# Two of a late turn's four sums and their low parts on GpSimd, and convolution operands in one run per partition

## The chip, the cores and the metric

The kernel runs on one core of a Trainium2 chip. The metric is device time in microseconds, the median of several runs. A core has five engines that work side by side, each in its own order: TensorE (PE; its weight loads are listed as PEld), VectorE (DVE), ScalarE (ACT), GpSimd (POOL) and SyncE (SP), which issues nearly all DMAs here.

## The reference

One layer of a hybrid backbone: an adaptive RMSNorm of x (2048 tokens of 1024) and of a context (256 tokens), one input projection, a bidirectional gated linear scan over eight heads and a gated short convolution beside each other, an output projection and a final norm. Cut to what matters:

```python
h = rmsnorm(x, norm_w) * (1 + scale) + shift
p = h @ w_in                      # 1024 x 9216: 5 parts for the scan, 4 for the convolution
q, v, kf, gf, kb, gb = hgrn_prep(p[..., :HG_COLS], lb_f, lb_b)
o, _, _ = bidir_scan(q, kf, kb, v, gf, gb, s_f, s_b)   # s_f, s_b from the context
y_hg = hgrn_out(o, gate, onorm_w)
h_, bg, cg, gate2 = the other four parts of p
y_cv = bg * conv3(cg * h_, w) * silu(gate2)
y = concat(y_hg, y_cv) @ w_out
out = rmsnorm(x + gate * y, final_norm_w)
```

## The kernel before

**Products.** A float32 product is made from fp16 operands, each split into a high part (the value cast to fp16) and a low part (the value less the high part). Per 128 rows of the contraction TensorE makes three matmuls: high by high, high by low, low by high (L930 to L932 in `seven`). A product of 2 x 2 blocks is made from seven products of blocks instead of eight. The moving operands of the seven are `OPS`: B11, T1, T2, B21, T3, B22, T4, where T1 = b12 - b11, T2 = b22 - T1, T3 = b22 - b12 and T4 = b21 - T2, and b11 to b22 are blocks of the normalised rows, 256 tokens wide. The results go to four banks (sa, sb and others) and are evacuated by ScalarE (`p` and `u`, L937) and VectorE (`f`, `b` and others, L941).

**Turns.** The tokens come in four groups of 512 (`GW`; `HW` is half of it). Of each group the rows are normalised, transposed by TensorE (L274) and scaled; then a *turn* makes operands of them, one step per k of 0 to 3, each with the 128 features k of the upper and of the lower half. Groups 2 and 3 get *whole* turns (`turn`, `combine` with `whole`), which make all seven operands. Groups 0 and 1 are first used plain, as undivided high and low parts, and their rows `h` are kept in DRAM (`Xd`); the T operands come later, in *late* turns (`late_turn`), which load the rows again as `ha` and `hb` and make T1 to T4. There are eight whole turns, between 88 and 196 us of the profiled execution, and eight late ones, between 196 and 336 us. `ht` holds T1 and T2 side by side; T3 is written over b12 in `ha`, T4 over b21 in `hb`.

`store2` splits one or two operands: a cast to the high part (`cast`, on ScalarE at L303 or on GpSimd at L301, as its caller says), a subtraction on VectorE for the low part (L321), and a DMA of the pair tile `hp...` to DRAM by SyncE (L324, L326). The list `low` collects these subtractions so that another group's normalisation can be ordered behind them (`follow`). `prefetch` loads operands of a group from DRAM into the tiles `hop...` (L1389), once all four late turns of that group have been recorded.

**What sets the order.** The program is recorded as a row of units of matmuls. Beside the units run steps (turns, levels of the scan, norms), which `run` and `tick` spread over the matmuls by weights in the table `PACE`. A scheduler then orders each engine's instructions, and tiles come free by their pools. The scan of one head goes through levels: per level ScalarE makes a rearranged copy `km` of K (L601) and GpSimd one of Q, `qm` (L608; one buffer); VectorE updates K and Q (L485, L492); TensorE multiplies them into A (L631, L650), which ScalarE and GpSimd copy on (L661, L665).

**Convolution units.** From about 1335 us on, 28 units of 84 matmuls (2352) each cover two token groups at once: 512 columns, 256 from either group. Their operands `C0...` and `C1...` are loaded from `Hd` in DRAM by `load_C` (L986 to L993) into tiles that hold, for each of four k, the high and the low part of 512 columns. Later the same tiles hold the operands of w_out (`wo_home`, `wo_at`, `load_wo`).

Of the kernel before, what the change touches and what calls it, by code (L numbers as in the profile page):

```python
# [10 lines left out]
F16 = mybir.dt.float16  # L11
# [4 lines left out]
ALU = mybir.AluOpType  # L16
# [3 lines left out]
P = 128  # L20
# [5 lines left out]
GW = 512  # L26
NG = SEQ // GW
NCH = GW // P
HK = KT // 2
HW = GW // 2  # L30
# [30 lines left out]
def hybrid_layer(ctx: ExitStack, tc, x, cx, w_ada, b_ada, w_in, w_out, fnorm_w, small_d, masks, ident_d, sel_d, out):  # L61
# [179 lines left out]
    def norm_group(ntile, src, row0, m, nm, first_ops=None, space=q_tile):  # L241
# [72 lines left out]
        def store2(ops, k, row, eng):  # L314

            n2 = len(ops)
            pair = hp.tile([P, n2, 2, HW], F16, tag="pair", name=f"hp{ops[0]}_{nm}{k}", bufs=4)
            hi, lo = pair[:, :, 0], pair[:, :, 1]
            row = row.rearrange("p (a b) -> p a b", a=n2)
            cast(eng, hi, row)  # L320
            low.append(V.tensor_tensor(lo, row, hi, ALU.subtract))  # L321
            g = row0 // GW
            if n2 == 2:
                SY.dma_start(Hr[g][ops][:, :, k], pair)  # L324
            else:
                SY.dma_start(Hd[g][ops[0]][:, k], pair[:, 0])  # L326
# [30 lines left out]
        def combine(k, a, b, whole):  # L357
            b11, b12, b21, b22 = a[:, :HW], a[:, HW:], b[:, :HW], b[:, HW:]
            t = ring(f"ht_{nm}{k}")
            t1, t2 = t[:, :HW], t[:, HW:]  # L360
            V.tensor_tensor(t1, b12, b11, ALU.subtract)
            V.tensor_tensor(t2, b22, t1, ALU.subtract)
            store2(("T1", "T2"), k, t, S)
            V.tensor_tensor(b12, b22, b12, ALU.subtract)
            if whole:
                store2(("B11", "T3"), k, a, S)
                store2(("B21", "B22"), k, b, G)
            else:
                store2(("T3",), k, b12, S)
            V.tensor_tensor(b21, b21, t2, ALU.subtract)  # L370
            store2(("T4",), k, b21, G)

        return ([paced("load", lambda i=i: load(i)) for i in range(ntile)],
                [paced("square", lambda i=i: square(i)) for i in range(ntile)] + [paced("norm", norm)],
# [611 lines left out]
    def load_C(names, pool=None, tp=0):  # L986

        def one(o, j):
            if j == 0:
                C[tp][o] = (pool or ext.cr).tile([P, HK, 2, GW], F16, name=f"C{tp}{o}")  # L990
            SY.dma_start(C[tp][o][:, :, :, j * HW:(j + 1) * HW], Hd[2 * tp + j][o])

        return [lambda o=o, j=j: one(o, j) for o in names for j in range(2)]  # L993

# [64 lines left out]

    def wo_home(name, hl):  # L1060
        i = 2 * OPS.index(name) + hl
        return C[i // 7][OPS[i % 7]]

    def wo_at(name, hl, k):
        return wo_home(name, hl)[:, k // 2, k % 2, :]

    def load_wo(lo_, hi_):

        for i in range(lo_, hi_):
            SY.dma_start(wo_home(OPS[i // 2], i % 2).rearrange("p a k n -> p (a k) n"), Wd[OPS[i // 2]][:, i % 2])  # L1070

    Gr = dp.tile([P, GW], F32, name="Gr", tag="Gr")

# [377 lines left out]
    ui = 0  # L1451

    def run(wi, units, steps):
# [20 lines left out]
        for un, (wk, kind, i, fn) in enumerate(units):  # L1474
# [36 lines left out]
            elif kind == "pair":  # L1511
                def pair_step(o, last_unit=ui == len(uses) - 1):
                    tick(2)
                    if o and last_unit and o != OPS[6]:
                        load_wo(7 + OPS.index(o), 8 + OPS.index(o))

                seven(w.ops.get, lambda o, hl, k, i=i: C[i][o][:, k, hl, :], HK, GW, f"{ui}", pair_step,
                      w.sx[:, 0:1], ring, retire, *fn(w))
            else:
                def step(o, final=final):  # L1520
                    tick(1)
                    if o and final:
                        freed[0] += 1
                        prefetch()

                seven(w.ops.get, lambda o, hl, k: hop[gw][o][:, k, hl, :], HK, HW, f"{ui}", step,
                      w.sx[:, 0:1], u_tile, retire, *fn(w))
# [157 lines left out]
```

## Time and profile before

| | us |
|---|---|
| median of 3 runs | 2150.0 (2148.01 to 2152.14) |
| profiled execution | 2151.83 |
| its span | 2150.1 |
| TensorE busy | 2073.2 (96% of the span) |
| TensorE's weight loads busy | 1466.0 (68%) |
| VectorE busy | 1645.8 (77%) |
| ScalarE busy | 1192.2 (55%) |
| GpSimd busy | 191.8 (9%) |

The profiled execution's time is the span and 1.7 us around it. The mean granted clock of TensorE is 0.994 of full speed. The shares are means over the whole program; what VectorE, ScalarE and GpSimd do in a stretch, and what TensorE waits for there, is read from that stretch (the rows further down). A wait is listed by the waiting instruction and the one that ended last before it could start.

### The profile page before, as it was taken

The page shows a single profiled execution, that of the slowest core. Times are in us where ns is not written, and L with a number is a line of the kernel's source. Part 1 is how long each engine was busy: PE and PEld are TensorE (multiplying, and loading weights), DVE is VectorE, ACT ScalarE, POOL GpSimd, SP SyncE. Part 2 cuts the span into 40 slices and gives each one's busy share as a digit, 9 for nine tenths or more (in the row PEclk, how much of TensorE's full clock was granted, in tenths as well). Part 3 has the DMA queues.
Part 4 walks back from the last instruction along what each step waited for, and adds up shares of the span by engine and source line. Part 5 has one row for each costly group of instructions (what it writes and reads, how often), then busy time and mean ns, then how long its engine had stood idle before and what let it go on. Part 6 is the DMA issues. An engine that isn't in the chain of part 4 may idle for free.

```text
span 2150.1 us, 53050 instructions
## 1 busy us (share of the span) xinstructions
PE 2073.2 (96%) x22111; PEld 1466.0 (68%) x22111; DVE 1645.8 (77%) x3413; ACT 1192.2 (55%) x2406; POOL 191.8 (9%) x272
## 2 busy tenths in 40 slices
PE   5988999999999999999999999999999999999998
PEld 2877878888888888888888887444444444444443
DVE  6787988878778787788687887678778656687775
ACT  7965666757567666576676654354445423333332
POOL 0121111111111110111110100000000000000000
PEclk9999999999999999999999999999999999999999
DMA  9567533442344233424543458933442105642421
GB/s 356 191 207 265 178 126 134 137 158 72 114 129 146 97 114 109 153 81 142 194 131 127 130 165 260 285 108 110 134 149 93 54 23 196 206 143 92 137 79 59
DMA packets 185798, 311.02 MB, mean 145 GB/s; under 512 B 13010, under 2 KB 114770, under 8 KB 183764
## 3 DMA queue, kind: packets, MB, share of 16 engines
q1 hardware_dynamic: 183396, 303.68, 42.9%
q8 instruction: 173, 2.83, 0.5%
q10 hardware_dynamic: 2160, 3.93, 0.5%
q14 instruction: 69, 0.57, 0.1%
HBM read 240.19 MB, written 67.37 MB: 143 GB/s over the span
## 4 chain that ended last, share of the span: by engine, by line
PE 65%; DVE 18%; ACT 7%; DMA 4%; issue 3%; POOL 1%; SPq 0%; POOLq 0%; ACTq 0%; DVEq 0%
PE sa L930 8%; PE sa L932 8%; PE sa L931 8%; PE sb L930 4%; PE sb L932 4%; PE sb L931 4%; PE sa_o L930 2%; PE sa_o L931 2%; PE sa_o L932 2%; DVE Q L492 2%; PE sc L930 2%; PE sc L931 2%; PE sc L932 2%; DVE K L485 2%; PE T L681 2%
## 5 line engine op out<-in xcount | busy, mean ns | idle before, releaser
L931 PEld LDWEIGHTS <-e_p 128*128 128x128 f16 x1332 | 130.4, 98 | 59.8 <-issue 10.3
L930 PEld LDWEIGHTS <-e_p 128*128 128x128 f16 x1332 | 130.4, 98 | 54.0 <-issue 1.1
L601 ACT ACTIVATE km<-K 128x512 f32<-128x512 f32 x192 | 129.6, 675 | 67.2 <-DVE K L485 61.1
L932 PEld LDWEIGHTS <-e_p 128*128 128x128 f16 x1332 | 130.3, 98 | 51.4
L485 DVE TENSOR_TENSOR K<-K,tot 128x512 f32<-128x512 f32 x192 | 132.2, 689 | 42.9 <-ACT km L601 25.3
L492 DVE TENSOR_TENSOR Q<-Q,tot 128x512 f32<-128x512 f32 x192 | 132.5, 690 | 34.9 <-POOL qm L608 19.5
L608 POOL COPY qm<-Q 128x512 f32<-128x512 f32 x96 | 80.8, 842 | 794.4 <-DVE Q L492 778.7
L931 PEld LDWEIGHTS <-whib_p 128*128 128x128 f16 x888 | 86.9, 98 | 42.1 <-issue 8.8
L930 PEld LDWEIGHTS <-whib_p 128*128 128x128 f16 x888 | 86.8, 98 | 36.7 <-issue 0.8
L930 PEld LDWEIGHTS <-whia_p 128*128 128x128 f16 x888 | 87.0, 98 | 35.7 <-DMA hop3B<-Hd3B 2.3
L932 PEld LDWEIGHTS <-wloa_p 128*128 128x128 f16 x888 | 87.0, 98 | 34.2
L931 PEld LDWEIGHTS <-whia_p 128*128 128x128 f16 x888 | 87.0, 98 | 33.9 <-issue 1.5
L932 PEld LDWEIGHTS <-wlob_p 128*128 128x128 f16 x888 | 86.8, 98 | 34.0
L157 ACT ACTIVATE e_p<-ws_p,sc_p 128x512 f16<-128x512 f32 x108 | 77.5, 718 | 54.9 <-DVE ws_p L444 42.0
L665 POOL COPY A<-Ac 32x128 f32<-32x128 f32 x128 | 77.2, 603 | 128.3 <-ACT A L661 110.6
L853 ACT ACTIVATE cv<-c,small 128x512 f32<-128x512 f32 (+1 forms) x36 | 24.2, 673 | 106.8 <-DVE c L871 61.1
L937 ACT ACTIVATE u<-sa,sx_w 128x256 f32<-128x256 f32 (+1 forms) x111 | 58.1, 524 | 43.5 <-PE sa L932 34.7
L937 ACT ACTIVATE p<-sa,sx_w 128x256 f32<-128x256 f32 (+1 forms) x111 | 57.4, 517 | 39.9 <-PE sa L932 39.8
L158 DVE SCALAR_TENSOR_TENSOR e_p<-ws_p,sc_p,e_p 128x512 f16<-128x512 f32 x108 | 79.4, 750 | 0.0
L409 ACT ACTIVATE junk<-ws_p 128x1024 f16<-128x1024 f32 x72 | 75.7, 1052 | 6.5 <-DMA ws_p<-in_w_in 6.3
L1596 POOL TENSOR_TENSOR x_o<-x_o,fw 128x512 f32<-128x512 f32 x1 | 1.3, 1262 | 868.0 <-ACT junk L1587 868.0
L937 ACT ACTIVATE p<-sb,sx_w 128x256 f32<-128x256 f32 (+1 forms) x111 | 57.8, 521 | 30.8 <-PE sb L932 28.0
(858 smaller groups left out, 7036.3 us busy)
## 6 DMA issues: line engine op xcount, KB each, us to landing
ws_p<-in_w_in SPq DMA_DIRECT2D x72, 512.0 KB, 4.3
y_o<-yT SPq DMA_DIRECT2D x32, 512.0 KB, 4.3
xt_x<-in_x SPq DMA_DIRECT2D x16, 512.0 KB, 6.2
wa<-in_w_ada SPq DMA_DIRECT2D x16, 512.0 KB, 10.2
Gd<-zs SPq DMA_DIRECT2D x32, 256.0 KB, 2.7
sg<-Gd SPq DMA_DIRECT2D x32, 256.0 KB, 4.4
wos<-in_w_out SPq DMA_DIRECT2D x32, 256.0 KB, 5.0
yT<-y SPq DMA_DIRECT2D x32, 256.0 KB, 2.9
```

The source lines that it names most:

```text
L157: S.activation(hi, src, AF.Copy, scale=st[:, 0:1])
L158: V.scalar_tensor_tensor(lo, src, st[:, 0:1], hi, ALU.mult, ALU.subtract)
L409: S.activation(junk.rearrange("p (k n) -> p k n", k=KT), stage[i], AF.Abs, accum_out=r)
L485: V.tensor_tensor(m, m, sub(cur, nb + 1, [[2, np_], [-(nb + 1), 2], [0, B]]), ALU.mult)
L492: V.tensor_tensor(m, m, sub(cur, 1, [[2, np_], [nb - 1, 2], [0, B]]), ALU.mult)
L601: S.activation(sub(s.km, 0, [[2 * B, n // (2 * B)], [B, 2], [1, B]]), mix(s.K, n, B, n // (2 * B)), AF.Copy)
L608: G.tensor_copy(sub(qm, 0, [[2 * B, n // (2 * B)], [B, 2], [1, B]]), mix(s.qf, n, B, n // (2 * B)))
L665: G.tensor_copy(A3[js, :, js], s.Ac[js])
L930: PE.matmul(ps, hi[:, k], rh, start=start and k == 0, stop=False, skip_group_check=not start)
L931: PE.matmul(ps, hi[:, k], right(name, 1, k), start=False, stop=False, skip_group_check=not start)
L932: PE.matmul(ps, lo[:, k], rh, start=False, stop=k == nk - 1, skip_group_check=not start)
L937: last_keep.append(S.activation(r, ps, AF.Copy, scale=sx))
```

## The change

In `combine`, a late turn makes T3 and T4 on GpSimd (`eng`); a whole turn makes them on VectorE as before. T4's high part is always cast by ScalarE. In `store2`, the low part of an operand that is stored alone (T3 and T4 of a late turn, T4 of a whole one) is subtracted on GpSimd, and it is no longer in the list `low`. The tiles `C` hold the two token groups behind each other ([P, 2, HK, 2, HW] in place of [P, HK, 2, GW]), so that one load is one run of 4 KB per partition in place of eight runs of 512 B; the matmuls' moving operand is then two stretches of 256 columns. The homes of w_out's operands are the same bytes under another view.

```diff
@@ -318,7 +318,10 @@
             hi, lo = pair[:, :, 0], pair[:, :, 1]
             row = row.rearrange("p (a b) -> p a b", a=n2)
             cast(eng, hi, row)
-            low.append(V.tensor_tensor(lo, row, hi, ALU.subtract))
+            if n2 == 2:
+                low.append(V.tensor_tensor(lo, row, hi, ALU.subtract))
+            else:
+                G.tensor_tensor(lo, row, hi, ALU.subtract)
             g = row0 // GW
             if n2 == 2:
                 SY.dma_start(Hr[g][ops][:, :, k], pair)
@@ -361,14 +364,15 @@
             V.tensor_tensor(t1, b12, b11, ALU.subtract)
             V.tensor_tensor(t2, b22, t1, ALU.subtract)
             store2(("T1", "T2"), k, t, S)
-            V.tensor_tensor(b12, b22, b12, ALU.subtract)
+            eng = V if whole else G
+            eng.tensor_tensor(b12, b22, b12, ALU.subtract)
             if whole:
                 store2(("B11", "T3"), k, a, S)
                 store2(("B21", "B22"), k, b, G)
             else:
                 store2(("T3",), k, b12, S)
-            V.tensor_tensor(b21, b21, t2, ALU.subtract)
-            store2(("T4",), k, b21, G)
+            eng.tensor_tensor(b21, b21, t2, ALU.subtract)
+            store2(("T4",), k, b21, S)
 
         return ([paced("load", lambda i=i: load(i)) for i in range(ntile)],
                 [paced("square", lambda i=i: square(i)) for i in range(ntile)] + [paced("norm", norm)],
@@ -987,8 +991,8 @@
 
         def one(o, j):
             if j == 0:
-                C[tp][o] = (pool or ext.cr).tile([P, HK, 2, GW], F16, name=f"C{tp}{o}")
-            SY.dma_start(C[tp][o][:, :, :, j * HW:(j + 1) * HW], Hd[2 * tp + j][o])
+                C[tp][o] = (pool or ext.cr).tile([P, 2, HK, 2, HW], F16, name=f"C{tp}{o}")
+            SY.dma_start(C[tp][o][:, j], Hd[2 * tp + j][o])
 
         return [lambda o=o, j=j: one(o, j) for o in names for j in range(2)]
 
@@ -1059,15 +1063,15 @@
 
     def wo_home(name, hl):
         i = 2 * OPS.index(name) + hl
-        return C[i // 7][OPS[i % 7]]
+        return C[i // 7][OPS[i % 7]].rearrange("p j k l n -> p (j k l n)").rearrange("p (k n) -> p k n", n=GW)
 
     def wo_at(name, hl, k):
-        return wo_home(name, hl)[:, k // 2, k % 2, :]
+        return wo_home(name, hl)[:, k, :]
 
     def load_wo(lo_, hi_):
 
         for i in range(lo_, hi_):
-            SY.dma_start(wo_home(OPS[i // 2], i % 2).rearrange("p a k n -> p (a k) n"), Wd[OPS[i // 2]][:, i % 2])
+            SY.dma_start(wo_home(OPS[i // 2], i % 2), Wd[OPS[i // 2]][:, i % 2])
 
     Gr = dp.tile([P, GW], F32, name="Gr", tag="Gr")
 
@@ -1514,7 +1518,7 @@
                     if o and last_unit and o != OPS[6]:
                         load_wo(7 + OPS.index(o), 8 + OPS.index(o))
 
-                seven(w.ops.get, lambda o, hl, k, i=i: C[i][o][:, k, hl, :], HK, GW, f"{ui}", pair_step,
+                seven(w.ops.get, lambda o, hl, k, i=i: C[i][o][:, :, k, hl, :], HK, GW, f"{ui}", pair_step,
                       w.sx[:, 0:1], ring, retire, *fn(w))
             else:
                 def step(o, final=final):
```

In the fences below, the number behind a name is the tile's; line numbers of the changed kernel are three higher from L325 and four higher from L364 on. First GpSimd's queue at the first two late turns (k = 0 and 1 of the group `x1`), before:

```order
L608 COPY qm1_0_2_2732<-Q_0_2_2411 128x512
L608 COPY qm3_0_2_2847<-Q_0_2_2411 128x512
L301 TENSOR_SCALAR hpT4_x10_2635<-hb_x10_2619 128x256
L301 TENSOR_SCALAR hpT4_x11_2840<-hb_x11_2824 128x256
L608 COPY qm5_0_2_2970<-Q_0_2_2411 128x512
L665 COPY A_0_2_3029<-Ac_0_2_2695 32x4x32 x4
```

and of the change:

```order
L612 COPY qm1_0_2_2732<-Q_0_2_2411 128x512
L368 TENSOR_TENSOR ha_x10_2618<-hb_x10_2619,ha_x10_2618 128x256
L612 COPY qm3_0_2_2847<-Q_0_2_2411 128x512
L374 TENSOR_TENSOR hb_x10_2619<-hb_x10_2619,ht_x10_2622 128x256
L324 TENSOR_TENSOR hpT3_x10_2630<-ha_x10_2618,hpT3_x10_2630 128x256
L324 TENSOR_TENSOR hpT4_x10_2635<-hb_x10_2619,hpT4_x10_2635 128x256
L368 TENSOR_TENSOR ha_x11_2823<-hb_x11_2824,ha_x11_2823 128x256
L374 TENSOR_TENSOR hb_x11_2824<-hb_x11_2824,ht_x11_2827 128x256
L324 TENSOR_TENSOR hpT3_x11_2835<-ha_x11_2823,hpT3_x11_2835 128x256
L612 COPY qm5_0_2_2970<-Q_0_2_2411 128x512
L324 TENSOR_TENSOR hpT4_x11_2840<-hb_x11_2824,hpT4_x11_2840 128x256
L669 COPY A_0_2_3029<-Ac_0_2_2695 32x4x32 x4
```

The two casts of T4 are gone; two sums (L368, L374) and two low parts (L324) per turn have come between the copies `qm1`, `qm3` and `qm5`.

ScalarE at the first late turn, before:

```order
L601 ACTIVATE km4_0_2_2850<-K_0_2_1859 128x512
L303 ACTIVATE hpT1_x10_2625<-ht_x10_2622 128x2x256
L303 ACTIVATE hpT3_x10_2630<-ha_x10_2618 128x256
L937 ACTIVATE p1_17_2864<-sa_17_2807,sx_w2_690 128x256
L542 ACTIVATE f_0_3_2573<-sa_16_2575,sx_w0_482 128x256
L523 ACTIVATE f_0_3_2573<-f_0_3_2573,lb_125,lb1_126 128x512
L538 ACTIVATE f_0_3_2573<-f_0_3_2573 128x512
L524 ACTIVATE K_0_3_2574<-f_0_3_2573 128x512
L523 ACTIVATE f_0_3_2573<-f_0_3_2573,lb_125,lb1_126 128x512
```

and of the change (`f_0_3` are evacuations and updates of the scan's gates, `p1_17` an evacuation of bank sa):

```order
L605 ACTIVATE km4_0_2_2850<-K_0_2_1859 128x512
L303 ACTIVATE hpT1_x10_2625<-ht_x10_2622 128x2x256
L303 ACTIVATE hpT3_x10_2630<-ha_x10_2618 128x256
L303 ACTIVATE hpT4_x10_2635<-hb_x10_2619 128x256
L542 ACTIVATE f_0_3_2573<-f_0_3_2573 128x512
L941 ACTIVATE p1_17_2864<-sa_17_2807,sx_w2_690 128x256
L527 ACTIVATE f_0_3_2573<-f_0_3_2573,lb_125,lb1_126 128x512
L546 ACTIVATE f_0_3_2573<-sa_16_2575,sx_w0_482 128x256
L528 ACTIVATE K_0_3_2574<-f_0_3_2573 128x512
L303 ACTIVATE hpT1_x11_2830<-ht_x11_2827 128x2x256
```

A cast of T4 stands behind that of T3, the three casts of the second turn have moved up behind K, and `p` stands behind one of the instructions on `f_0_3`.

VectorE at the same turn, before (`Q` is the scan's update, `Ac` its masked copy, `f_0_3` an evacuation of bank sb):

```order
L361 TENSOR_TENSOR ht_x10_2622<-ha_x10_2618 128x256
L492 TENSOR_TENSOR Q_0_2_2411<-Q_0_2_2411,tot_0_2_2639 128x64x2x4
L362 TENSOR_TENSOR ht_x10_2622<-hb_x10_2619,ht_x10_2622 128x256
L364 TENSOR_TENSOR ha_x10_2618<-hb_x10_2619,ha_x10_2618 128x256
L370 TENSOR_TENSOR hb_x10_2619<-hb_x10_2619,ht_x10_2622 128x256
L639 COPY_PREDICATED Ac_0_2_2695<-mask_127,A2_0_2_2755 128x128
L321 TENSOR_TENSOR hpT1_x10_2625<-ht_x10_2622,hpT1_x10_2625 128x2x256
L321 TENSOR_TENSOR hpT3_x10_2630<-ha_x10_2618,hpT3_x10_2630 128x256
L321 TENSOR_TENSOR hpT4_x10_2635<-hb_x10_2619,hpT4_x10_2635 128x256
L639 COPY_PREDICATED Ac_0_2_2695<-mask_127,A2_0_2_2755 128x128
L941 SCALAR_TENSOR_TENSOR f_0_3_2573<-sb_16_2607,sx_w0_482,u2_16_2709 128x256
```

and of the change:

```order
L364 TENSOR_TENSOR ht_x10_2622<-ha_x10_2618 128x256
L496 TENSOR_TENSOR Q_0_2_2411<-Q_0_2_2411,tot_0_2_2639 128x64x2x4
L365 TENSOR_TENSOR ht_x10_2622<-hb_x10_2619,ht_x10_2622 128x256
L643 COPY_PREDICATED Ac_0_2_2695<-mask_127,A2_0_2_2755 128x128
L945 SCALAR_TENSOR_TENSOR f_0_3_2573<-sb_16_2607,sx_w0_482,u2_16_2709 128x256
L643 COPY_PREDICATED Ac_0_2_2695<-mask_127,A2_0_2_2755 128x128
L322 TENSOR_TENSOR hpT1_x10_2625<-ht_x10_2622,hpT1_x10_2625 128x2x256
L496 TENSOR_TENSOR Q_0_2_2411<-Q_0_2_2411,tot_0_2_2639 128x32x2x8
```

Two of the four sums and two low parts have left, and the evacuation at L941 (now L945) stands ahead of T1 and T2's low part.

## Rows read from the trace of the kernel before

**Rows 1.** stretches of the program; the columns are in its first line

```profile
core 0: us, PE busy (x) PEld busy (x) DVE busy (x) ACT busy (x) POOL busy (x), PEclk, DMA share, GB/s
88.00:196.00 108.00, 97.15 (x1338) 80.63 (x1337) 88.19 (x196) 70.88 (x126) 22.78 (x31) 0.98 0.65 222
196.00:336.00 140.00, 129.33 (x1977) 111.92 (x1975) 123.81 (x288) 90.93 (x207) 25.34 (x35) 1.00 0.53 174
...
1280.00:1400.00 120.00, 118.27 (x793) 77.38 (x792) 79.74 (x162) 50.90 (x117) 0.00 (x0) 1.00 0.83 259
```

**Rows 2.** TensorE's waits, 88 to 196: line, waited for, total us, times, longest

```profile
PE A L631 <- POOL qm L608: 2.1, 3, 1.3
...
PE xT_x L274 <- DVE xt_x L267: 2.0, 2, 1.5
PE sb L930 <- DVE f L941: 1.7, 1, 1.7
```

**Rows 3.** TensorE's waits, 196 to 336

```profile
PE A L650 <- POOL qm L608: 2.7, 2, 1.5
PE A L631 <- POOL qm L608: 1.5, 3, 0.8
PE sb L930 <- DVE f L941: 1.3, 1, 1.3
PE sa L930 <- DVE f L941: 1.2, 1, 1.2
PE sa L930 <- ACT p L937: 1.1, 1, 1.1
```

**Rows 4.** timeline of VectorE: start us, duration us, line, operation

```profile
93.53 0.83 DVE L362 TENSOR_TENSOR ht_x<-h_x,ht_x 128x256 f32<-128x256 f32 x1
...
203.35 0.41 DVE L321 TENSOR_TENSOR hpT_x<-ha_x,hpT_x 128x256 f16<-128x256 f32 x1
203.69 0.41 DVE L321 TENSOR_TENSOR hpT_x<-hb_x,hpT_x 128x256 f16<-128x256 f32 x1
```

**Rows 5.** line 321, what ended VectorE's idle time before it: us, times

```profile
  POOL hpT_x L301: 1.9, 7
```

**Rows 6.** timeline of GpSimd

```profile
93.31 0.79 POOL L301 TENSOR_SCALAR hpB_x<-h_x 128x512 f16<-128x512 f32 x1 [12.62 <-ACT h_x L296]
...
207.37 1.52 POOL L301 TENSOR_SCALAR hpT_x<-hb_x 128x256 f16<-128x256 f32 x1 [4.47 <-DVE s_p L424]
...
317.38 1.66 POOL L301 TENSOR_SCALAR hpT_x<-hb_x 128x256 f16<-128x256 f32 x1 [3.21 <-DVE hb_x L370]
...
2132.68 1.26 POOL L1596 TENSOR_TENSOR x_o<-x_o,fw 128x512 f32<-128x512 f32 x1 [868.04 <-ACT junk L1587]
```

**Rows 7.** line 301, GpSimd's casts: ns min, median and max, starts, form

```profile
L301 POOL TENSOR_SCALAR hpB_x<-h_x x8: 617/774/909, 93.3 to 173.2; 128x512 f16<-128x512 f32 x8
L301 POOL TENSOR_SCALAR hpT_x<-h_x x8: 400/405/1119, 98.2 to 179.9; 128x256 f16<-128x256 f32 x8
```

**Rows 8.** timeline of ScalarE

```profile
201.77 0.63 ACT L303 ACTIVATE hpT_x<-ht_x 128x512 f16<-128x512 f32 x1 [3.46 <-DVE ht_x L362]
202.31 0.40 ACT L303 ACTIVATE hpT_x<-ha_x 128x256 f16<-128x256 f32 x1
202.61 0.46 ACT L937 ACTIVATE p<-sa,sx_w 128x256 f32<-128x256 f32 x1
```

**Rows 9.** timeline of SyncE's queue, the issue of one load

```profile
321.00 0.80 SPq L1389 DMA_DIRECT2D hop7T<-Hd0T  x2
```

**Rows 10.** tile hop7B, TensorE's first reader: ns min/median/max, first and last start

```profile
L930 PE MATMUL sa<-hop7B,whia_p x20: 272/273/273, 332.7 to 391.6; 128*128 128x256 f16 x20
```

**Rows 11.** timeline of TensorE, the first pair unit

```profile
1335.83 0.38 PE L930 MATMUL sa<-C0B,whia_p 128*128 128x512 f16 x1 [0.89 <-DVE b L941]
...
1336.26 0.38 PE L932 MATMUL sa<-C0B,wloa_p 128*128 128x512 f16 x1
```

**Rows 12.** TensorE's line 631 by form: count, busy us, mean ns, idle

```profile
L631 PE MATMUL A<-Q,km 128*32 128x32 f32 x3072 | 48.8, 204 | 4.3 <-DVE Q L492 3.1 <-ACT km L601 0.5 <-DVE Q L567 0.4
L631 PE MATMUL A<-qm,km 128*32 128x32 f32 x2048 | 29.6, 199 | 9.7 <-POOL qm L608 9.7
```

## The prediction

> **What bounds the kernel now.** I read the table of stretches first. TensorE is busy 97.15 of the 108 us from 88 to 196, and 129.33 of the 140 us from 196 to 336; from 1280 to 1400 it is busy 118.27 of 120 [rows 1]. So TensorE is the bound, and a change on other engines is worth at most the idle time it can close: 10.9 us and 10.7 us in the two early stretches, where the operand turns are, and 1.7 us where the convolutions' operands come in. VectorE is nearly as full there: 88.19 of 108 and 123.81 of 140 [rows 1].
>
> Then I read what TensorE waits for. In the first stretch: 2.1 us for GpSimd's copy `qm`, 2.0 us for the scaled x tile, 1.7 us for `f` (VectorE's evacuation of bank sb) [rows 2]. In the second: 2.7 and 1.5 us for `qm`, 1.3 and 1.2 us for `f`, 1.1 us for `p`, which ScalarE evacuates [rows 3]. VectorE, GpSimd's `qm` and ScalarE's `p` are therefore what the change has to be weighed on: it takes work from the first and lays it in front of the other two.
>
> **What leaves VectorE.** A late turn loses four instructions of 128x256 on VectorE (two sums, two low parts), a whole turn one (T4's low part): 8 x 4 + 8 x 1 = 40. They stand 0.34 us apart (203.35 to 203.69) [rows 4], so 13.6 us. VectorE's waits for GpSimd's casts, 1.9 us in seven places [rows 5], go with them: 15.5 us.
>
> **What comes to GpSimd.** Sixteen casts go, 40 two-input instructions of 128x256 come. The trace has none of that shape. The nearest are a two-input one of 128x512 with 1.26 us [rows 6] and casts of 128x512 and 128x256 with at least 0.617 and 0.400 us [rows 7]. The casts give 0.18 us that doesn't scale; (1.26 - 0.18) / 2 + 0.18 = 0.72 us, which I take for one alone. The ends are 0.63 us (half of 1.26) and, beside a busy VectorE, 0.72 + 1.12 = 1.84 us, since one cast of 0.40 took 1.52 at 207.37 [rows 6]. GpSimd's load over the 248 us is 22.8 + 25.3 = 48.1 us [rows 1]; less 16 x 0.40 and with 40 x 0.72 or 40 x 1.1 it is 71 or 86 us. It does not become the bound by its sum, only by its order.
>
> **What the two engines cost each other.** The rows show either one losing. At 93.53 a VectorE subtraction took 0.83 us instead of 0.41 while GpSimd ran a cast [rows 4, 6]; at 207.37 it was GpSimd that lost 1.12 us. GpSimd's time alone grows by 40 x 0.72 - 16 x 0.40 = 22.4 us. If VectorE loses none of that it gains the whole 15.5 us; if it loses all, it is 6.9 us worse off. I take a quarter, 5.6 us, because in VectorE's fullest stretch it was GpSimd that lost: VectorE keeps some 10 us.
>
> The Trainium skill (SBUF — State Buffer, section Who interferes with whom) speaks against the change: a VectorE instruction with two SBUF inputs and a GpSimd instruction that reads SBUF exclude each other, and the one that starts second is blocked until the first ends. By that rule either engine can lose, as the rows above show; with GpSimd always first VectorE would lose the 22.4 us, which is the second rival below.
>
> **What of it lies on TensorE's path**, place by place.
> - The x tile (1.5 us at the longest [rows 2]): four whole turns lie ahead of it on VectorE, which give it 4 x 0.34 us and two of the waits for casts. I take 1.0 us, ends 0 and 1.5.
> - `f` in the first stretch (1.7 us [rows 2]): two whole turns ahead. I take 0.7 us, ends 0 and 1.0.
> - The two `f` of the second stretch (1.3 and 1.2 us [rows 3]): each stands directly behind a late turn, and the order shows the first now ahead of T1 and T2's low part. 4 x 0.34 = 1.36 us covers each wait. I take all 2.5 us, ends 1.2 and 2.5.
> - `qm`: it now stands behind differences and low parts. Between qm3 and qm5 of the first late turns the order has six two-input instructions, 4.3 us at 0.72 and 6.6 us at 1.1; Q comes earlier too. For the wait of 1.5 us before qm5 of that segment I take a gain of 0.5 us (ends: gain 1.5, loss 1.5). At the last late turns one cast of 1.66 us already holds up a `qm` [rows 6]; there I take a loss of 0.5 us (ends: gain 0.5, loss 3).
> - `p`: ScalarE runs in order, and the casts of T3 and T4 now stand together behind T1 and T2's, ahead of `p`. Before, that cast began at 201.77, T3's at 202.31, `p` at 202.61 [rows 8]. Now T4's cast waits for two subtractions of GpSimd in a row. I take 1.0 us at the first late turn, where TensorE already waited for `p` (ends 0 and 1.9), and nothing at the seven others, where ScalarE has gaps; at worst 1 us each.
>
> Sum: -1.0 - 0.7 - 2.5 - 0.5 + 0.5 + 1.0 = -3.2 us. The best ends give -7, the worst +12.
>
> **Edits I cost at nothing.** The stores of T3 and T4 now wait for GpSimd, and SyncE's queue stands behind them. The loads that follow the last of them, `hop7T`, were issued at 321.00 [rows 9], and TensorE first reads that set's first tile at 332.7 [rows 10], 11.7 us later, against at most 3 us of delay; the largest waits of this stretch name no DMA [rows 3]. Were that room gone, each microsecond of delay would be one of the sum. T4's cast in whole turns costs ScalarE 8 x 0.3 us in gaps.
>
> **The convolutions' operands.** Loads get one run of 4 KB per partition in place of eight of 512 B. No wait of TensorE for them is in the trace; what it waits for at the turn to the pair units is VectorE's `b`, 0.9 us [rows 11]. Faster loads are hidden. The reading side could cost: 2352 matmuls of 512 columns now take their columns from two stretches. The nearest rows are the small matmuls whose moving operand is broken up (`Q`, 204 ns) or whole (`qm`, 199 ns) [rows 12]. By their means a broken operand costs between nothing and 2.5%, which on 2352 x 0.215 = 506 us (they start 0.43 us per two [rows 11]) would be 12.7 us. I take nothing: those means hold waits too, and the runs here are 256 long, those there 1 to 16.
>
> **The sum.** The profiled execution took 2151.8 us (span 2150.1), the median of the runs is 2150.0. 2151.8 - 3.2 = 2148.6 for such an execution, and 2150.0 - 3.2, so 2147 us, for the median.
>
> **Rivals.**
> 1. ScalarE's queue turns the sign. Place: the three casts in a row in each late turn, with `p`, K, kT or A behind them. Price: where GpSimd needs about 1.1 us or more for a difference, T4's cast is over 1.5 us later than before; if five of eight turns pass 1.6 us on, that is +8, less the 3 us above: 2155 us. Against it: ScalarE is busy only 90.93 of 140 us [rows 1]. For it: GpSimd is slow just where VectorE is full.
> 2. GpSimd holds VectorE: VectorE is 6.9 us worse off, and about two thirds reach TensorE where it waits for VectorE's results: 2155 us. Against it: 207.37; for it: 93.53.
> 3. A wash: the gain at `f` is given back at `qm` and `p`: 2150 us. Each of those is a direct successor of moved work.
> 4. More gain: VectorE is behind most of the 13.6 us of waits in [rows 2, 3], `qm` too, since Q is VectorE's. If all of VectorE's 10 us count until TensorE is full, about 8 us: 2142 us.
> 5. Matmuls from two stretches are slower: 2147 + 12.7 = 2160 us.
>
> **How the numbers follow.** My forecast has 0.45 (own range 2144 to 2149.5), rival 4 0.18, rival 3 0.17, rival 1 0.09, rival 2 0.07, rival 5 0.04. A measurement of this kernel tells about 0.2% from no change, 4.3 us. Faster by more than that: rival 4 and two fifths of the forecast, 0.36. Slower: nearly all of rivals 1, 2 and 5, 0.18. The rest, 0.46, is within it. The range of 8 in 10 goes from 2140.5, a little past rival 4, to 2156, past rivals 1 and 2, and leaves out rival 5.
>
> **What would show it.** VectorE's busy time from 88 to 336 falls by 8 to 11 us; GpSimd's rises by 22 to 38. The waits for `f` in the late stretch are gone, the one for `p` is above 1.1 us, and those for `qm` stay within 1 us in sum. TensorE's matmuls on C0 and C1 keep 0.38 us, and the time after 336 is unchanged. If two-input instructions take over 1.3 us on average, or TensorE waits for `p`, `kT` or `A` in several late turns, the forecast is wrong on the slow side; if the wait for the x tile and both `f` vanish and `qm` shrinks too, on the fast side.

## The result and the profile after

The changed kernel takes 2155.0 us (median of 15 runs, 2152.3 to 2159.5), before 2150.0 (15 runs): ratio 1.0026, 95% interval 1.0019 to 1.0034. A second set of runs of the same kernel gave 1.0032 (1.0022 to 1.0041). It is slower by 4 to 9 us; 2147 was forecast. The profiled execution took 2154.55 us (span 2152.8).

First the table of stretches of the changed kernel, with the columns of [rows 1]:

```profile
core 0: us, PE busy (x) PEld busy (x) DVE busy (x) ACT busy (x) POOL busy (x), PEclk, DMA share, GB/s
88.00:196.00 108.00, 96.61 (x1331) 79.92 (x1330) 87.17 (x187) 72.97 (x133) 29.61 (x31) 0.98 0.67 226
196.00:336.00 140.00, 127.65 (x1954) 110.97 (x1953) 122.21 (x254) 91.78 (x213) 48.01 (x59) 0.99 0.50 163
1280.00:1400.00 120.00, 118.29 (x795) 77.67 (x792) 79.20 (x161) 50.85 (x118) 0.00 (x0) 1.00 0.72 259
```

VectorE has 9 and 34 instructions less in the two early stretches than in [rows 1], and is busy 1.0 and 1.6 us less. GpSimd is busy 6.8 and 22.7 us more. In the stretch of the convolutions' turn the engines are as before; the DMA engines move the same 259 GB/s in 0.72 of their time in place of 0.83 (0.73 in e1_layout below, which has the new loads alone), and no wait gets shorter by it.

Fixed stretches don't hold the same work once one kernel is late, so the next two rows, one of either kernel, end where TensorE first reads the tile `hop7B`, behind the last late turn: 332.7 us before [rows 10], 335.7 after. They hold 3282 and 3280 matmuls. Before:

```profile
88.00:332.70 244.70, 223.18 (x3282) 189.55 (x3281) 209.88 (x479) 159.26 (x329) 48.12 (x66) 0.99 0.58 194
```

and after:

```profile
88.00:335.70 247.70, 223.96 (x3280) 190.63 (x3279) 209.08 (x439) 164.45 (x345) 77.62 (x90) 0.99 0.58 190
```

This is the central reading. VectorE does 40 instructions less and is busy 209.08 us in place of 209.88: 13.6 us of work went, 0.8 us was won. GpSimd rose by 29.5 us, from 48.12 to 77.62.

The two engines' timelines in the first late turns say where the 12.8 us went. VectorE after (start, duration, line, operation):

```profile
199.11 0.95 DVE L365 TENSOR_TENSOR ht_x<-hb_x,ht_x 128x256 f32<-128x256 f32 x1
...
201.69 1.16 DVE L496 TENSOR_TENSOR Q<-Q,tot 128x512 f32<-128x512 f32 x1
202.77 0.89 DVE L364 TENSOR_TENSOR ht_x<-ha_x 128x256 f32<-128x256 f32 x1
```

GpSimd after, the same time:

```profile
199.04 0.73 POOL L368 TENSOR_TENSOR ha_x<-hb_x,ha_x 128x256 f32<-128x256 f32 x1 [3.26 <-DMA hb_x<-Xd]
...
201.18 1.12 POOL L324 TENSOR_TENSOR hpT_x<-ha_x,hpT_x 128x256 f16<-128x256 f32 x1
202.26 1.12 POOL L324 TENSOR_TENSOR hpT_x<-hb_x,hpT_x 128x256 f16<-128x256 f32 x1
```

A subtraction of 128x256 that takes VectorE 0.41 us [rows 4] takes 0.95 and 0.89 beside a GpSimd subtraction, and the update of Q, 128x512, takes 1.16. Where the loss fell is seen by form, here the update of Q from 88 to 336 us, before and after (count, busy us, mean ns, idle before):

```profile
L492 DVE TENSOR_TENSOR Q<-Q,tot 128x512 f32<-128x512 f32 x36 | 24.8, 688 | 1.4 <-POOL qm L608 1.1 <-PE A L631 0.3
L496 DVE TENSOR_TENSOR Q<-Q,tot 128x512 f32<-128x512 f32 x36 | 29.1, 809 | 2.6 <-POOL qm L612 1.6 <-PE A L635 1.0
```

The same 36 updates are busy 4.3 us longer, and those of K go from 699 to 770 ns on the mean. So what was taken from VectorE were sums and low parts of the turns, and what was lengthened are in good part the scan's updates, which TensorE's product A stands behind. GpSimd's instructions take 0.73 where VectorE starts second, 1.12 where GpSimd is held too. By form over the whole program (count, busy us, mean ns, idle before):

```profile
L324 POOL TENSOR_TENSOR hpT_x<-h_x,hpT_x 128x256 f16<-128x256 f32 x8 | 10.6, 1330 | 24.8 <-ACT hpT_x L303 24.7
L324 POOL TENSOR_TENSOR hpT_x<-hb_x,hpT_x 128x256 f16<-128x256 f32 x8 | 8.5, 1060 | 0.0
L324 POOL TENSOR_TENSOR hpT_x<-ha_x,hpT_x 128x256 f16<-128x256 f32 x8 | 8.4, 1050 | 2.2 <-ACT hpT_x L303 2.2
L368 POOL TENSOR_TENSOR ha_x<-hb_x,ha_x 128x256 f32<-128x256 f32 x8 | 8.0, 995 | 21.8 <-DMA hb_x<-Xd 17.4 <-DVE ht_x L364 3.4 <-DVE e_p L158 0.6
L374 POOL TENSOR_TENSOR hb_x<-hb_x,ht_x 128x256 f32<-128x256 f32 x8 | 7.6, 950 | 1.5 <-DVE ht_x L365 1.5
```

The mean of all 40 is 1.08 us; 0.72 was my estimate for one alone.

What TensorE waits for after the change, 88 to 196 us:

```profile
PE sa L934 <- DMA hop3B<-Hd3B: 2.6, 1, 2.6
PE xT_x L274 <- DVE xt_x L267: 1.5, 2, 1.0
PE sb L934 <- DVE f L945: 1.4, 1, 1.4
PE A L635 <- ACT km L605: 1.1, 1, 1.1
```

and 196 to 336 us:

```profile
PE sb L934 <- ACT p L941: 2.0, 1, 2.0
PE A L635 <- DVE Q L496: 1.7, 4, 0.8
PE A L635 <- POOL qm L612: 1.7, 2, 1.2
PE ss_p L145 <- ACT rb_p L417: 1.6, 1, 1.6
PE sa L934 <- DVE f L945: 1.4, 1, 1.4
PE A L654 <- POOL qm L612: 1.2, 2, 0.9
PE A L661 <- DVE Q L496: 0.8, 1, 0.8
```

Against [rows 2, 3]: the x tile gave 0.5 us, `f` 0.3 in the first stretch and 1.1 in the second, `qm` 1.3 in the second. In their place stand VectorE's Q (1.7 and 0.8 us, before 0.3), ScalarE's `p` (2.0, before 1.1), the weights' statistics `rb_p` (1.6) and `km` (1.1). The wait for the load `hop3B` was there before too, 2.1 us. All that the wait lists name adds up to 20.7 us before and 23.6 after; by the engine waited for, GpSimd's part went from 6.3 to 4.3 us, VectorE's from 8.8 to 8.5, and ScalarE's from 3.5 to 8.2.

The longest, for `p`, shows how the gain turns into a wait. ScalarE after:

```profile
206.93 0.40 ACT L303 ACTIVATE hpT_x<-ha_x 128x256 f16<-128x256 f32 x1
207.23 0.40 ACT L303 ACTIVATE hpT_x<-hb_x 128x256 f16<-128x256 f32 x1
207.54 0.61 ACT L528 ACTIVATE K<-f 128x512 f32<-128x512 f32 x1
208.06 0.46 ACT L941 ACTIVATE p<-sb,sx_w 128x256 f32<-128x256 f32 x1
```

and TensorE:

```profile
208.56 0.27 PE L934 MATMUL sb<-hop3B,e_p 128*128 128x256 f16 x1 [2.02 <-ACT p L941]
```

`f` came early (200.18 in place of 204.22), so TensorE ran 3 us ahead of before. It then stood before the next bank: `p` was evacuated 0.5 us earlier than before (208.06 in place of 208.60), not 3, since it waits its turn behind two casts of operands and a K, on a ScalarE that works at the pace of VectorE's and GpSimd's results.

The granted clock after, in stretches of 2 us around its two falls:

```profile
186.00:188.00 2.00, 1.74 (x9) 1.25 (x10) 0.00 (x0) 0.00 (x0) 0.00 (x0) 0.50 0.99 291
188.00:190.00 2.00, 2.00 (x14) 1.55 (x13) 0.00 (x0) 0.47 (x1) 0.00 (x0) 0.67 1.02 385
...
206.00:208.00 2.00, 0.55 (x5) 0.34 (x4) 2.00 (x5) 2.00 (x5) 0.91 (x2) 1.00 0.00 0
208.00:210.00 2.00, 1.05 (x22) 0.69 (x22) 2.00 (x5) 2.00 (x5) 1.39 (x3) 0.95 0.59 197
210.00:212.00 2.00, 2.00 (x10) 1.39 (x10) 2.00 (x6) 2.00 (x4) 0.37 (x1) 0.50 0.24 74
212.00:214.00 2.00, 2.00 (x53) 1.43 (x51) 2.00 (x4) 0.55 (x2) 0.00 (x0) 0.69 0.81 228
```

TensorE was busy 0.55 and 1.05 of 2 us before the second fall, and waited 2.6 us for `hop3B` ahead of the first. 0.50 is the lower of its two levels, 1.2 in place of 2.4 GHz. The four rows of 186 to 190 and 210 to 214 cost (0.50 + 0.33 + 0.50 + 0.31) x 2 = 3.3 us; before there was one fall in these stretches, at 138 to 142 us (0.59 and 0.56), 1.7 us. Waits (2.9 us more) and clock (1.6) would make it 4.5 us later at the end of the late turns; the two rows that end at `hop7B` say 3.0. The rest of 1.5 us I can't put on a row. The first pair unit reads C0 here at 1336.3 us (1335.83 before [rows 11]), with the same duration:

```profile
L934 PE MATMUL sa<-C0B,whia_p x56: 377/379/379, 1336.3 to 1794.4; 128*128 128x512 f16 x56
```

So 2.5 of the 3.0 us had been handed back on the way, mostly near 1035 us, and a wait of 2.1 us for a `p` at 1839 us came later. Both scatter: the same turns read C0 at 1341.3 and 1339.1 us in two other profiles (e2_turns, e11_again below), the turns of before at 1334.0 (e1_layout), and the wait at 1839 is there in e5_cast and not in e2_turns. From the first read of C0 to the end every profile of the layer takes 814.2 to 814.4 us, but the four that have this wait (the one here, e5_cast, e7_whole, e11_again), which take 1 to 2 us more. Over the profiles `hop7B` is read at 335.7, 341.2 and 336.2 us with the changed turns, and at 332.7 and 331.1 with those of before: 5.8 us between the means, as large as the whole difference of the medians. By these means the loss arises before the late turns' end. Added up over stretches of 2 us, 3.4, 6.8 and 1.7 us were lost there to the lower clock with the changed turns, 1.7 and 0 with those of before: 3.1 of the 5.8 us, in profiles that scatter as much as that.

### The profile page after: what moved, and what is told of

It is laid out like the page before. It is cut to its first block, busy times and chain, and to the rows that moved or that the text cites. A ratio compares the mean times of both kernels' runs of the same rounds, so it can differ in the third digit from the quotient of the medians.

```text
span 2152.8 us, 53037 instructions
## 1 busy us (share of the span) xinstructions
PE 2073.0 (96%) x22111; PEld 1467.9 (68%) x22111; DVE 1645.0 (76%) x3373; ACT 1197.1 (56%) x2422; POOL 221.0 (10%) x296
## 4 chain that ended last, share of the span: by engine, by line
PE 59%; DVE 12%; ACT 6%; DMA 2%; issue 2%; POOL 1%; POOLq 0%; SPq 0%; ACTq 0%; DVEq 0%
PE sa L934 7%; PE sa L936 7%; PE sa L935 7%; PE sb L934 3%; PE sb L936 3%; PE sb L935 3%; PE sa_o L934 2%; PE sa_o L935 2%; PE sa_o L936 2%; PE sc L934 2%; PE sc L935 2%; PE sc L936 2%; PE A L635 1%; PE T L685 1%; DVE Q L496 1%
## 5 line engine op out<-in xcount | busy, mean ns | idle before, releaser
L941 ACT ACTIVATE u<-sa,sx_w 128x256 f32<-128x256 f32 (+1 forms) x111 | 58.1, 524 | 45.0 <-PE sa L936 35.6
L941 ACT ACTIVATE p<-sa,sx_w 128x256 f32<-128x256 f32 (+1 forms) x111 | 57.4, 518 | 42.3 <-PE sa L936 42.3
L157 ACT ACTIVATE hiS_o<-y_o,sc_y 128x1024 f16<-128x1024 f32 x32 | 36.8, 1149 | 71.7 <-PE sa_o L935 31.6
```

The source lines that it names most:

```text
L157: S.activation(hi, src, AF.Copy, scale=st[:, 0:1])
L941: last_keep.append(S.activation(r, ps, AF.Copy, scale=sx))
```

## The experiments

Theory 1: GpSimd and VectorE hold each other up whenever both work on SBUF; what VectorE was relieved of, it loses in longer instructions. Theory 2: the engines wait for GpSimd's results in order, ScalarE above all. Theory 3: the convolutions' new layout costs it. Medians and ratios to before on the same chip, 95% intervals; the last column is TensorE's first read of `hop7B` in the one profile (before: 332.7).

| run | 128x256 subtractions on GpSimd | us | ratio | `hop7B`, us |
|---|---|---|---|---|
| e1_layout | 0 | 2149.9 | 1.0004 (0.9995 to 1.0013) | 331.1 |
| e2_turns | 40 | 2155.1 | 1.0028 (1.0017 to 1.0039) | 341.2 |
| e3_sums | 16 | 2152.4 | 1.0017 (1.0009 to 1.0026) | 334.5 |
| e4_lows | 24 | 2152.6 | 1.0014 (1.0006 to 1.0023) | 336.2 |
| e5_cast | 0 | 2149.2 | 0.9995 (0.9986 to 1.0004) | 329.9 |
| e6_unread | 40, beside VectorE's own | 2170.2 | 1.0099 (1.0085 to 1.0113) | 351.6 |
| e7_whole | 8 | 2149.2 | 1.0001 (0.9992 to 1.0009) | 333.3 |
| e9_tiny | 40 of 128x4 | 2148.8 | 1.0003 (0.9993 to 1.0013) | 332.8 |
| e10_nocast | 0, and no casts | 2145.1 | 0.9983 (0.9974 to 0.9992) | 329.4 |
| e11_again | 40 (the change) | 2156.1 | 1.0032 (1.0022 to 1.0041) | 336.2 |
| e12_qm | 0, no casts, no `qm` | 2149.5 | 0.9998 (0.9989 to 1.0007) | 324.5 |
| e13_early | 0, no casts, no early `qm` | 2143.1 | 0.9975 (0.9966 to 0.9984) | 325.1 |

**The two halves of the change.** e1_layout has the diff's parts in `load_C`, `wo_home` and the pair units' operand alone, e2_turns those in `store2` and `combine` alone.

> Only the convolutions' operands are laid out in one run per partition; the turns are those of before, and the order of every engine is the same. If the loss of 5 us (2155.0 against 2150.0) came from the convolution side (matmuls that read two stretches, or loads that land earlier and collide with others), this kernel shows it: 2155 us, and matmuls on C0 and C1 start more than 0.43 us per two. The theories that put the loss in the turns expect 2150 us, within 2 us of before, and the pair units unchanged.

> Only the turns are changed (two sums and the low parts of operands stored alone on GpSimd, T4's cast on ScalarE); the convolutions' loads are those of before. All theories that put the loss in the turns expect the whole of it: 2154 to 2156 us. The convolution theory expects 2150 us or a little less.

The turns are the whole of it, and the layout costs nothing: matmuls that read two stretches of 256 take as long as before. Theory 3 falls.

**The cast, and unread work.** e5_cast is before with T4's cast on ScalarE:

```diff
-            store2(("T4",), k, b21, G)
+            store2(("T4",), k, b21, S)
```

> Before, with one word changed: T4's cast always on ScalarE. Sums and low parts stay on VectorE, so GpSimd loses 16 casts and gains nothing. Theory 1 (GpSimd and VectorE hold each other up): no more holding than before, VectorE's 1.9 us of waits for GpSimd's casts go; VectorE busy from 196 to 336 stays near 124 us or falls by 1 to 2; 2146 to 2150 us. Theory 2 (ScalarE's queue: three casts in a row delay p, K, kT behind them): this kernel has the same casts on ScalarE as the change, so a good part of the loss shows: 2152 to 2155 us, with waits of TensorE for p or km of 1 us or more.

e6_unread adds to it subtractions on GpSimd that nobody reads:

```diff
             store2(("T1", "T2"), k, t, S)
+            for _ in range(1 if whole else 4):
+                G.tensor_tensor(unread, t1, t2, ALU.subtract)
```

> The kernel with T4's cast on ScalarE, and 40 subtractions of 128x256 on GpSimd beside it (4 in each late turn, 1 in each whole one) whose result nobody reads. VectorE, ScalarE, TensorE and SyncE have the same instructions in the same order as without them, and VectorE does all sums and low parts itself. Theory 1 (holding): the 40 take 0.7 to 1.1 us each, and VectorE's busy time from 88 to 336 grows by about as much as it failed to shrink in the change, 0.3 us per GpSimd instruction, so 10 to 14 us; the time is 4 to 10 us above that of the kernel without them. Theory 2 (ScalarE behind GpSimd's results): no result of the 40 is waited for except by way of qm's place in GpSimd's queue, so the time is within 2 us of that of the kernel without them.

The cast alone makes no difference, so three casts in a row on ScalarE are not what costs. The unread work costs 21 us, far more than I expected of either theory, though no engine waits for a result of it. Up to the first read of `hop7B`, e5_cast and then e6_unread (columns as above):

```profile
88.00:329.90 241.90, 222.79 (x3278) 188.87 (x3276) 207.87 (x476) 163.76 (x345) 39.83 (x50) 0.99 0.58 195
```

```profile
88.00:351.60 263.60, 230.12 (x3276) 192.72 (x3274) 223.97 (x475) 164.56 (x345) 73.93 (x90) 0.96 0.54 179
```

VectorE has the same work in both and is busy 16.1 us longer (I had written 10 to 14), 0.40 us for each of the 40. One of its subtractions (L374, 0.41 us alone) takes 0.88 on the mean of the eight late turns. And TensorE's mean granted clock is 0.96 in place of 0.99: (0.04 x 263.6) - (0.01 x 241.9) = 8 us of the 21.7 by which `hop7B` is later. That term I had left out. A further part is GpSimd's queue itself: at 336.5 us the copy `qm` stood behind four unread subtractions, and TensorE waited 3.7 us for it. The other long waits for `qm` (12.1 us in all up to `hop7B`, 5.7 in e5_cast) end on copies that waited for VectorE's Q.

**Place or duration.** e9_tiny is e6_unread with operands of 128x4:

```diff
-                G.tensor_tensor(unread, t1, t2, ALU.subtract)
+                G.tensor_tensor(unread[:, :4], t1[:, :4], t2[:, :4], ALU.subtract)
```

> The kernel with 40 unread subtractions on GpSimd, each of 128x4 in place of 128x256. Order, places in GpSimd's queue and waits are the same; only the time in which GpSimd reads and writes is taken away. Theory 1 (holding): back to the kernel without them, 2148 to 2151 us (2149.2 measured without, 2170.2 with the full size). If it was the places in GpSimd's queue, the semaphores or the tile ht held longer, most of the 20 us stays: 2160 us or more.

The same instructions in the same order, each waiting for the same results, and the 20 us are gone, VectorE's 16 us with them:

```profile
88.00:332.80 244.80, 224.78 (x3280) 190.35 (x3279) 207.11 (x479) 164.62 (x345) 50.55 (x90) 0.99 0.58 194
```

The tiny subtractions still occupy GpSimd for 14.5 us (361 ns each, 950 at full size), and VectorE loses nothing by them. So what VectorE loses goes with the time in which GpSimd reads and writes. This run also frees GpSimd's queue sooner, so it does not by itself take that part away from the 21 us; the wait of 3.7 us is what shows of it.

**Sums or low parts.** e3_sums has the `eng` lines, e4_lows the branch in `store2`. Both have T4's cast on ScalarE, e3_sums too, though its expectation says GpSimd; so e5_cast, which has that cast alone, is the kernel to set both against.

> Only the sums T3 and T4 of the late turns on GpSimd (16 subtractions); all low parts on VectorE, T4's cast in late and whole turns as before on GpSimd. Theory 1 (holding): 16 of 40 instructions make two fifths of the loss: 2151 to 2153 us. Theory 2 (ScalarE and VectorE wait for GpSimd's results): the sums are what casts and low parts wait for, so nearly all of the 5 us shows here, 2154 us or more.

> Only the low parts of operands stored alone on GpSimd (24 subtractions: T3 and T4 of the late turns, T4 of the whole ones) and T4's cast on ScalarE; all sums on VectorE. Only stores wait for a low part. Theory 1 (holding): three fifths of the loss, 2152 to 2154 us, and VectorE's two-input instructions stretched wherever a GpSimd subtraction starts first. Theory 2 (waiting for GpSimd's results): no loss, 2148 to 2150 us.

The sums are waited for by casts and low parts, the low parts only by stores; both cost about 3 us (ratios 1.0017 and 1.0014), and the two together about the change's loss. Theory 2 had all of it in the sums. e3's interval would allow it up to 5.6 us, e4's excludes its zero. In e4_lows, where only stores wait for GpSimd's subtractions, TensorE waits 6.2 us for ScalarE's results and 5.4 for VectorE's Q up to `hop7B`, 3.1 and 1.7 in e5_cast: ScalarE comes late there without a cast that waits for GpSimd. Per instruction the sums cost more (3.7 us by the ratio for 16, 3.0 for 24), but the intervals overlap; that waiting has a part in the sums is neither shown nor excluded. The stores behind GpSimd cost nothing that shows: the only load that TensorE waits for is `hop3B`, 2.0 us in e4_lows, 2.6 in e5_cast.

**The whole turns alone.** e7_whole takes the low part of T4 to GpSimd, and its cast to ScalarE, in whole turns only.

> Only the whole turns are changed: T4's low part on GpSimd, its cast on ScalarE; late turns as before. 8 subtractions come to GpSimd, 8 casts of it go. Theory 1 (holding, 0.4 us of VectorE lost per GpSimd subtraction beside it, 0.34 us won for each instruction taken away): a wash, 2148 to 2151 us.

A wash, as expected.

**The price by itself.** e8_micro runs both engines alone and side by side, in one execution.

> Nothing of the layer: VectorE and GpSimd alone and side by side, in fifteen phases; 24 instructions of VectorE and 16 of GpSimd of 128x256 each (128x512 where VectorE's are wide). Theory 1 (holding): side by side, two-input VectorE instructions take their own time plus GpSimd's: 24 x 0.34 + 16 x 0.7 = 19 us for the pair of sums or low parts, in place of the longer of 8 and 11 us; with one input (a bank as the other, or one operand) VectorE is not or less lengthened. A rival, a common limit of the memory, lengthens all forms alike. A cast on GpSimd holds like a subtraction by the first, less by the second.

Alone, by form (mean ns behind the busy time): a VectorE sum, VectorE with one operand, VectorE with a PSUM bank as one of two operands, a GpSimd sum:

```profile
L56 DVE TENSOR_TENSOR vo<-va 128x256 f32<-128x256 f32 x24 | 10.5, 437 | 0.8
L62 DVE TENSOR_SCALAR vo<-va 128x256 f32<-128x256 f32 x24 | 7.1, 294 | 0.8
L65 DVE SCALAR_TENSOR_TENSOR vo<-ps,va 128x256 f32<-128x256 f32 x24 | 10.2, 424 | 0.8
L71 POOL TENSOR_TENSOR go<-ga 128x256 f32<-128x256 f32 x13 | 9.4, 722 | 1.0
```

Side by side, in the same order of VectorE's forms, and last a VectorE sum beside GpSimd's casts:

```profile
L56 DVE TENSOR_TENSOR vo<-va 128x256 f32<-128x256 f32 x24 | 16.7, 694 | 0.8
L71 POOL TENSOR_TENSOR go<-ga 128x256 f32<-128x256 f32 x16 | 12.7, 791 | 1.2
L62 DVE TENSOR_SCALAR vo<-va 128x256 f32<-128x256 f32 x24 | 14.5, 606 | 0.8
L65 DVE SCALAR_TENSOR_TENSOR vo<-ps,va 128x256 f32<-128x256 f32 x24 | 10.2, 424 | 0.8
L71 POOL TENSOR_TENSOR go<-ga 128x256 f32<-128x256 f32 x16 | 11.6, 724 | 1.2
L56 DVE TENSOR_TENSOR vo<-va 128x256 f32<-128x256 f32 x24 | 11.4, 475 | 0.8
```

Beside GpSimd's sums a VectorE sum goes from 437 to 694 ns: 24 x 0.257 = 6.2 us for 16 GpSimd instructions, 0.39 each, while one of GpSimd's grows by only 0.07 (722 to 791). So the two don't take turns at full length, as I had expected (19 us; from VectorE's first to its last it was 17.45), but it is VectorE that pays. The form with one operand is lengthened too (294 to 606 ns), against my expectation; with a bank as the other operand both keep their time (424 ns in either case; 722 and 724). A common limit of the memory would have lengthened all. GpSimd's casts cost VectorE little here: 475 ns. In the kernel they cost more: up to `hop7B` VectorE is busy 2.0 us less than before in e5_cast, for 16 of them gone, and 4.2 us less in e10_nocast, for 24.

**Taking more off GpSimd.** If theory 1 holds, before is improved in the other direction. e10_nocast moves GpSimd's remaining casts of these turns to ScalarE:

```diff
-                store2(("B21", "B22"), k, b, G)
+                store2(("B21", "B22"), k, b, S)
...
-            store2(("T4",), k, b21, G)
+            store2(("T4",), k, b21, S)
```

> All sums and low parts on VectorE as before, and all casts of late turns and of whole ones on ScalarE: GpSimd does nothing in the turns of groups 2, 3 and in the late ones. Theory 1 (holding) expects a little less than before: VectorE is held by 24 casts less, each worth at most 0.1 us when they run back to back beside it, and its 1.9 us of waits for GpSimd's casts go: 2146 to 2149 us. Theory 2 (ScalarE's queue) expects it slower: 2151 us or more, as eight casts of 128x512 (0.62 us) come to ScalarE besides.

It is faster than before by 3.7 us (ratio 0.9983), with 2145.1 us about 1 us below what theory 1 expected. VectorE, with all its sums and low parts, is busy 205.67 us up to the first read of `hop7B` at 329.4, less than the 209.08 after the change.

e11_again is the change once more:

> The changed kernel once more, for a second profile and more runs. Theory 1: 2154 to 2156 us, VectorE's busy time from 88 to 336 as little below that of before as in the first profile (0 to 4 us for 42 instructions), and again two stretches or more between 88 and 336 in which the granted clock is about 0.5, where the kernel without GpSimd's subtractions has one or none.

The time came as expected, and so did VectorE: 209.2 us busy from 88 to 336, 2.8 below [rows 1]. The clock did not: only one fall in this profile's stretch, so one profile's count of them carries little.

e12_qm goes on with the scan's copies:

```diff
-            G.tensor_copy(sub(qm, ...), mix(s.qf, ...))
+            S.activation(sub(qm, ...), mix(s.qf, ...), AF.Copy)
```

> The kernel without casts on GpSimd in the turns (2145.1 us), and the scan's copies qm (96 of 128x512) on ScalarE in place of GpSimd as well, so that beside VectorE's updates of K and Q nothing of GpSimd is left but small copies of 32x128 and the first groups' casts. Theory 1 (holding): qm took 0.84 us on average on GpSimd, 0.61 where nothing held it; on ScalarE it takes some 0.6 us, and TensorE's waits for qm, 12.4 us over the whole program before the change, shrink by a third or more: 2138 to 2143 us. Theory 2 (ScalarE's queue): 96 x 0.6 = 58 us come to an engine that is 66% full between 88 and 336 us and stands in order; km, p and u come later by that, and the time is 2146 us or more.

A miss: 2149.5. Up to the late turns' end it gained 4.9 us over e10_nocast, and then lost all of it and 2.4 us more (in the profiles; by the ratios it ends 3 us behind). From 88 to 1336 us TensorE waits there for `qm` less, for ScalarE's `u` much more (e12_qm, then before):

```profile
PE sa L930 <- ACT u L937: 12.0, 18, 1.7
PE A L631 <- ACT qm L608: 4.4, 8, 1.7
```

```profile
PE A L631 <- POOL qm L608: 9.7, 13, 2.7
PE sa L930 <- ACT u L937: 3.6, 12, 0.6
```

So outside the turns ScalarE's queue decides, as theory 2 has it. e13_early keeps `qm` on ScalarE only until the last late turn is recorded:

```diff
+            if sum(late_done.values()) < 2 * HK:
+                S.activation(dst, src, AF.Copy)
+            else:
+                G.tensor_copy(dst, src)
```

> The kernel without casts on GpSimd in the turns, with the copies qm on ScalarE only as long as late turns are still to come (17 of 96 copies); after that qm is GpSimd's again. With all 96 on ScalarE TensorE was 4.9 us earlier at the end of the late turns (hop7B first read at 324.5 against 329.4 us) and had lost it all by 1300 us. Theory 1 (holding costs where VectorE is full, which is the stretch of the turns): the 4.9 us are kept, 2139 to 2142 us. Rival (the early gain is handed back later in any case, by loads or by the scan's own chain): hop7B still at 324 to 326 us, but 2144 to 2146 us at the end.

In the profiles it reads `hop7B` at 325.1 us, 4.3 ahead of e10_nocast, and is 3.1 ahead at the end. 2143.1 us lies between the two expectations, 2139 to 2142 and 2144 to 2146: a part of the gain is kept, a part is handed back. By its ratio of 0.9975 it is 5.4 us under before, and some 12 us under the change. It has the lowest median of all; under e10_nocast it is 1.7 us by the ratios, whose intervals overlap, so that the step from e10_nocast to e13_early is not shown by the times.

## Why the prediction was wrong

**The step that failed** is "What the two engines cost each other". I counted 13.6 us off VectorE rightly, and 1.9 us of waits for GpSimd's casts; then I took a quarter of GpSimd's growth as VectorE's loss, 5.6 us, and had it keep some 10. It lost 12.8 us and kept 0.8. My reason was one instant, 207.37 [rows 6], where GpSimd had lost; the row at 93.53 [rows 4, 6], where VectorE had, stood beside it. e8_micro shows which of the two is the rule when both are full: VectorE pays 0.39 us per GpSimd instruction of 0.72, GpSimd 0.07. In the kernel it was 12.8 / 40 = 0.32 against before, which has 16 more casts on GpSimd; against e5_cast, where these are gone too, it was (209.08 - 207.87 + 13.6) / 40 = 0.37, and by the same working 0.42 in e3_sums, 0.36 in e4_lows, 0.40 in e6_unread. At 0.39 the sum would have read 40 x 0.39 = 15.6 against 15.5 us: nothing kept.

The Trainium skill (SBUF — State Buffer, section Who interferes with whom) states that VectorE shares one pair of ports with GpSimd, takes it for a second SBUF input or in its faster one-input modes, and that whoever comes second is blocked. The rows of e8_micro agree on which forms are lengthened: two SBUF operands and the one-operand form are, an operand from a bank is not. On the size they do not: if either engine were blocked for whole instructions, the two sums would take 24 x 0.437 + 16 x 0.722 = 22.0 us, and it was 17.45. I had cited the page and given it 0.07. The rival that rested on it, GpSimd holding VectorE, has the time right, 2155 us, but by luck, for the size of its term is not: VectorE came out even, not 6.9 us worse.

A VectorE that comes out even explains a time like that of before, not a longer one: in e1_layout it is busy 209.2 us as well, and `hop7B` is read there at 331.1. The rest is read from the waits and not shown by a run of its own: the lost time fell on Q and K, and TensorE came to wait where it had not before.

**The terms on TensorE's path.** The gains at the x tile (0.5 us of 1.0 taken), at the first `f` (0.3 of 0.7) and at the late `f` (1.1 of 2.5) are all about half or less; VectorE had won only 0.8 us ahead of them. `p` lost 0.9 us (2.0 against 1.1) where I had taken 1.0, by luck: the wait at the first late turn (for the matmul at 203.12 before) is gone, and the new one stands at the second late turn, where I had put nothing. `qm` gained 1.3 where I had put nothing, in the lists of 196 to 336. What was missing is the other side: with GpSimd on them, VectorE's updates of Q came late (from 196 to 336, 2.5 us of waits where 0.3 had been), and so did ScalarE's results (over both stretches 8.2 us in place of 3.5; 3.1 in e5_cast, which has the same casts on ScalarE). A sum over the waits that are there already does not see the new ones.

**The clock** was not in the sum at all. In the first profile after, either fall came behind a wait of TensorE (2.6 and 2.0 us) and cost 1.6 or 1.7 us; but e10_nocast waited 2.6 us for `hop3B` without a fall, and e9_tiny has two falls at the time of before. Over the profiles with none or 8 subtractions of full size on GpSimd (before, e1, e5, e7, e9, e10) `hop7B` is read at 329.4 to 333.3 us; with 16 to 40 of them in place of VectorE's at 334.5 to 341.2. How much of that is clock varies from one profile to the next (one fall in e11_again, two in the first profile), so its share of the 5 us stays open.

**What was right:** the convolutions' part costs nothing, and matmuls from two stretches keep their time; the bound, TensorE, and its waits in the early stretches as the place; 0.72 us for a GpSimd subtraction alone (722 ns). Rival 1, ScalarE's queue, is refused as the whole cause by e5_cast (the casts alone cost nothing) and e4_lows (3 us without a cast that waits for GpSimd), though it decides in e12_qm; its condition of about 1.1 us for a difference did come true (1.08 on the mean), and a part for it in the sums stays open. The chance of slower, 0.18, was too small by the weight of one disregarded row.

## What to carry to other kernels

Before moving elementwise work from VectorE to GpSimd, run the two instructions back to back beside each other, as e8_micro does, and take the longer durations as the price; one overlap in a trace can show either engine losing, as [rows 4, 6] did. Where VectorE is full, an instruction moved from it is paid back in what remains there, and what remains may lie nearer to the bound. The direction that helped here was the other one: casts went from GpSimd to ScalarE, which gave 3.7 us; copies too gave something by the profiles, but only in the stretch where VectorE is full and ScalarE is not. Unread extra work, and the same at a tiny size, tell contention from waiting for results in two runs; how long the extra work holds up its own queue has to be read from the waits.

## What the runs showed of the hardware that was not expected

- Back to back, VectorE bears nearly all of the cost: 0.39 us per GpSimd sum of 0.72, GpSimd 0.07.
- VectorE's one-operand multiply of 128x256 loses more in proportion (294 to 606 ns) than its sum (437 to 694).
- With one operand in PSUM there is no cost at all (424 ns in either case).
- 40 GpSimd instructions, 38 us of an idle engine's time, cost the program 21 us without one result being used; 40 of 128x4, 14.5 us of its time, cost nothing that shows (2148.8 us).
